# Row softmax on one core: two tiles loaded as one transfer, two stored as one, in a common block of DRAM rows

## The chip, the core and the metric

The kernel runs on one core of one Trainium2 chip; the other cores take no part. The metric is the device time in microseconds (us) from start to end of one execution.

## The reference

```python
def reference(x):                       # x: 16 x 1024 x 512, float32
    x_scaled = x / 2.0
    x_max = np.max(x_scaled, axis=-1, keepdims=True)
    exp_x = np.exp(x_scaled - x_max)
    return (exp_x / np.sum(exp_x, axis=-1, keepdims=True)).astype(np.float32)
```

That is 16,384 rows of 512 numbers, 2 KB a row, 33.55 MB in and 33.55 MB out. Each row is softmaxed by itself.

## The kernel before

The 128 partitions take 128 rows each. A partition's 128 rows are cut into ten tiles, numbered from 0, of 3, 5 and then eight times 15 rows (`TILES`, line 10: rows and the place in `arena`). `arena` is the only data buffer in SBUF, 98 rows per partition; load, exponential, product and store all work in place in it. The tiles 0 to 7 fill it, and the tiles 8 and 9 are laid over tiles 0 to 3 once those are stored.

Three lists say how tiles share DRAM and transfers. `BLOCKS` says which tiles share a block of DRAM rows: within a block of r rows per partition, partition p holds r rows one after the other (`dram`, line 78), so a tile's piece per partition is contiguous and the pieces of neighbouring partitions stand r rows apart. `LOADS` says which tiles are one load (line 130), `STORES` which are one store (line 153); before, `STORES` is `BLOCKS`. A transfer is 128 pieces, one per partition: 15 rows are 30,720 bytes, 30 rows are 61,440.

Who issues what:

- SP issues the load of tile 0, ACT's queue the loads of tiles 1 to 7, all in the first microseconds and without a wait. They run in that order.
- POOL issues the two late loads (`LATE`, line 18). It waits until the exponentials of all tiles before row 83, which are the tiles 0 to 6, are done (line 192, `TURN`), then for the first two stores (tiles 0 and 1, and tile 2) before it loads tile 8, and for the third (tile 3) before it loads tile 9; `LATE` maps a load's number to the numbers of the stores that it newly waits for.
- SP issues all stores in order (lines 229 to 233, `store` at line 150). Before the first it waits until tile 2 has been multiplied; before the second it waits until the first has landed; and each waits until the last tile in it has been multiplied. The landed stores set the semaphores that POOL waits for; the last but one sets `s_near`.

The computation does not subtract the maximum. ACT takes exp(x/2) of one row per partition per instruction, and adds up the row's sum on the way (line 222 for tile 0, line 292 in a loop over chunks of 5 rows for the others). It waits (line 156, `take`) for a count that PE passes on as each load lands (line 209). DVE forms reciprocals (line 182) and multiplies (line 185), 15 rows at a time, and 5 rows at a time in the last tile. At the end, all sums are tested to lie within bounds (POOL line 196, DVE lines 200 and 204, PE line 214); if one does not, a second program over the whole input runs, which it does not do for this input. SP's last waits (lines 277 and 278) are for the last stores.

So there is a load queue (ACT's, then POOL's) and a store queue (SP's), which meet in the same 16 DMA engines.

Of the kernel before, what the change touches and what calls it, by code (L numbers as in the profile page):

```python
# [10 lines left out]
    (3, 0), (5, 3), (15, 8), (15, 23), (15, 38), (15, 53), (15, 68), (15, 83), (15, 0), (15, 15),  # L11
]

BLOCKS = [(0, 1), (2,), (3,), (4,), (5,), (6, 7), (8, 9)]
LOADS = [(0,), (1,), (2,), (3,), (4,), (5,), (6,), (7,), (8,), (9,)]
STORES = BLOCKS

LATE = {8: (0, 1), 9: (2,)}
ARENA = 98

HEAD = [3]
# [11 lines left out]
def kernel(  # L33
# [36 lines left out]
    def span(ts):  # L70
        assert all(tiles[u][2] == tiles[t][2] + tiles[t][1] for t, u in zip(ts, ts[1:]))
        return tiles[ts[0]][0], sum(tiles[t][1] for t in ts), tiles[ts[0]][2]

    for part in (BLOCKS, LOADS, STORES):
        assert [t for ts in part for t in ts] == list(range(len(tiles)))
    loaded = [span(ts) for ts in LOADS]

    def dram(ap, ts):
        b, r, _ = span(ts)
        first, rows, _ = next(span(us) for us in BLOCKS if ts[0] in us)  # L80
        assert first <= b and b + r <= first + rows
        block = ap[first * P : (first + rows) * P].rearrange("(p r) d -> p r d", r=rows)
        return block[:, b - first : b - first + r]

    def sb(ts):
        _, r, at = span(ts)
        return arena[:, at : at + r, :]
# [18 lines left out]
    ld = [nc.alloc_semaphore(f"ld{k}") for k in range(len(loaded))]  # L106
    s_home = {k: nc.alloc_semaphore(f"s_home{k}") for k in LATE}
    s_near = nc.alloc_semaphore("s_near")
# [19 lines left out]
    def load(eng, k):  # L128
        ts = LOADS[k]
        eng.dma_start(out=sb(ts), in_=dram(xf, ts)).then_inc(ld[k], 16)  # L130

    stored_by = {j: s_home[k] for k, js in LATE.items() for j in js}
    for k, (_, r, at) in enumerate(loaded):
        over = {
            j for j, ts in enumerate(STORES)
            if any(
                u < LOADS[k][0] and tiles[u][2] < at + r and at < tiles[u][2] + tiles[u][1]
                for u in ts
            )
        }  # L140
        assert over <= {j for v, js in LATE.items() if v <= k for j in js}

    def landings(js):
        return 16 * len(list(js))

    near = len(STORES) - 2
    sem_of = {**stored_by, near: s_near}
    at_end = landings(j for j in range(len(STORES)) if j not in sem_of)

    def store(eng, j):  # L150
        ts = STORES[j]
        eng.wait_ge(s_mul, upto[ts[-1]])
        eng.dma_start(out=dram(of, ts), in_=sb(ts)).then_inc(sem_of.get(j, s_end), 16)
# [19 lines left out]
    def loads():  # L173
        for k in range(2, min(LATE)):
            load(nc.scalar, k)

    def program():
# [14 lines left out]
        nc.gpsimd.wait_ge(s_exp, starts.index(TURN))  # L192
        for k, js in LATE.items():
            nc.gpsimd.wait_ge(s_home[k], landings(js))
# [13 lines left out]

        for k, ts in enumerate(LOADS):
            nc.tensor.wait_ge(ld[k], 16).then_inc(  # L210
# [17 lines left out]

        nc.sync.wait_ge(s_mul, upto[STORES[FIRST][-1]])
        for j in range(len(STORES)):  # L230
            if j == FIRST:
                nc.sync.wait_ge(s_home[min(LATE)], landings(range(j)))
            store(nc.sync, j)
# [109 lines left out]
```

## Time and profile before

| | |
|---|---|
| median of three runs | 159.79 us (159.79 to 159.9) |
| the profiled execution: its time, its span | 159.81 us, 158.5 us |
| ACT busy | 80.4 us (51%) |
| DVE busy | 73.2 us (46%) |
| DMA records, bytes moved | 2448, 67.11 MB |
| load queue of ACT (q10) | 24.90 MB |
| store queue of SP (q1, with the load of tile 0) | 34.34 MB |
| load queue of POOL (q0) | 7.86 MB |

The span goes from the first to the last instruction of the core; the time has 1.3 us more around it. In the profile's lines PE is TensorE, DVE VectorE, ACT ScalarE, POOL GpSimd, SP SyncE; a q behind an engine's name is its sequencer, which issues transfers and waits. L130 is line 130 of the kernel. A row of 40 digits cuts the span, or the window asked for, in 40 equal slices; each digit is the busy share in tenths. A record (the profile says packet) is one piece of a transfer on one DMA engine.

### The profile page before, as it was taken

To read this page: it belongs to the slowest core of one execution; us is meant where nothing else is said; L and a number is where in the kernel's file an instruction comes from. 1 tells how busy PE (TensorE), PEld (TensorE's weight loads), DVE (VectorE), ACT (ScalarE), POOL (GpSimd) and SP (SyncE) were. 2 spreads that over 40 slices of the span, in tenths; PEclk is the share of its full clock that TensorE was granted. 3 is DMA by queue.
4 is the path that set the end of the run, shared out by engine and by line. 5 is a ranking of instruction groups with operands and counts; after the bars stand their busy time and mean duration, and the time that the engine had idled before them with its cause. 6 is when DMAs were issued, how large, how long until landed. Compare 5 with 4: busy or idle time off the path is not lost. (4 is left out here: it accounts for less than half of the span.)

```text
span 158.5 us, 654 instructions
## 1 busy us (share of the span) xinstructions
PE 0.2 (0%) x2; PEld 0.1 (0%) x2; DVE 73.2 (46%) x27; ACT 80.4 (51%) x257; POOL 2.2 (1%) x8
## 2 busy tenths in 40 slices
PE   0000000000000000000000000000000000000000
PEld 0000000000000000000000000000000000000000
DVE  0056003989989369459500991005964990000000
ACT  0690799999929938940399000894029900000000
POOL 0000000000000000000100010000000010000000
DMA  6999999999998999999999999999999996999695
GB/s 235 442 473 395 473 395 473 395 473 399 412 447 380 466 411 434 434 427 442 419 450 403 465 403 465 403 465 403 465 403 465 496 496 279 465 496 481 295 465 248
DMA packets 2448, 67.11 MB, mean 424 GB/s; under 512 B 272, under 2 KB 272, under 8 KB 400
## 3 DMA queue, kind: packets, MB, share of 16 engines
q1 hardware_dynamic: 1152, 34.34, 50.5%
q10 hardware_dynamic: 1008, 24.90, 36.9%
q0 software_dynamic: 288, 7.86, 11.5%
HBM read 33.55 MB, written 33.55 MB: 424 GB/s over the span
## 5 line engine op out<-in xcount | busy, mean ns | idle before, releaser
L292 ACT ACTIVATE arena<-arena x125 | 76.6, 614 | 41.4 <-ACTq L156 41.4
L185 DVE TENSOR_TENSOR arena<-arena,recip 128x7680 f32<-128x7680 f32 (+2 forms) x12 | 70.2, 5847 | 0.4
L182 DVE RECIPROCAL recip<-stats 128x15 f32<-128x15 f32 (+2 forms) x12 | 2.7, 224 | 56.8 <-ACT arena L292 48.3
L292 ACT ACTIVATION_READ_ACCUMULATOR arena<-arena x125 | 23.4, 187 | 0.0
L218 ACT ACT_TABLE_LOAD x1 | 1.3, 1283 | 4.7 <-issue 4.7
L130 POOL DMA_DIRECT2D arena<-in_x_dram x2 | 1.3, 630 | 89.1 <-DMA out_dram<-arena 89.1
L222 ACT ACTIVATE arena<-arena 128x512 f32<-128x512 f32 x3 | 1.9, 618 | 0.5 <-ACTq L156 0.5
L196 POOL TENSOR_SCALAR inside<-stats 128x128 f32<-128x128 f32 x1 | 0.6, 629 | 35.0 <-ACT arena L292 35.0
L222 ACT ACTIVATION_READ_ACCUMULATOR arena<-arena 128x1 f32 x3 | 0.6, 185 | 0.0
L214 PE MATMUL total<-ones,count 128*1 128x1 f32 x2 | 0.2, 164 | 130.3 <-DVE inside L200 130.3
L200 DVE SCALAR_TENSOR_TENSOR inside<-inside,stats 128x128 f32<-128x128 f32 x1 | 0.3, 283 | 0.0
L204 DVE TENSOR_SCALAR flag<-total 1x1 int32<-1x1 f32 x1 | 0.1, 145 | 0.3 <-PE total L214 0.3
L214 PEld LDWEIGHTS total<-ones,count 128*1 128x1 f32 x2 | 0.1, 80 | 130.3 <-DVE inside L200 130.3
L191 POOL MEMSET ones<- 128x1 f32 x1 | 0.1, 98 | 1.1 <-POOLq L41 1.1
L327 POOL MEMSET const-float32-0.0<- 128x1 f32 x1 | 0.1, 104 | 0.2 <-issue 0.2
L327 POOL MEMSET const-bfloat16-1.0<- 128x1 bf16 x1 | 0.1, 107 | 0.0
L327 POOL MEMSET const-uint8-127<- 128x1 uint8 x1 | 0.1, 107 | 0.0
L327 POOL MEMSET const-float32-1.0<- 128x1 f32 x1 | 0.1, 104 | 0.0
L200 DVE DVE_READ_ACCUMULATOR inside<-inside,stats 128x1 f32 x1 | 0.1, 82 | 0.0
## 6 DMA issues: line engine op xcount, KB each, us to landing
arena<-in_x_dram ACTq DMA_DIRECT2D x6, 3840.0 KB, 38.2
out_dram<-arena SPq DMA_DIRECT2D x4, 3840.0 KB, 45.9
out_dram<-arena SPq DMA_DIRECT2D x2, 7680.0 KB, 36.4
arena<-in_x_dram POOLq DMA_DIRECT2D x2, 3840.0 KB, 24.5
out_dram<-arena SPq DMA_DIRECT2D x1, 2048.0 KB, 19.0
arena<-in_x_dram ACTq DMA_DIRECT2D x1, 1280.0 KB, 7.3
arena<-in_x_dram SPq DMA_DIRECT2D x1, 768.0 KB, 6.3
```

What stands on the lines that cost most here:

```text
L130: eng.dma_start(out=sb(ts), in_=dram(xf, ts)).then_inc(ld[k], 16)
L182: nc.vector.reciprocal(out=recip[:, b : b + c], in_=stats[:, b : b + c])._wait_ge(s_exp, ks[-1] + 1).then_inc(s_rec, 1)
L185: nc.vector.tensor_mul(out=arena[:, a : a + c], in0=arena[:, a : a + c], in1=recip[:, b : b + c].unsqueeze(2).to_broadcast([P, c, D]),)._w ...
L191: nc.gpsimd.memset(ones[:, :], 1.0).then_inc(s_ones, 1)
L196: nc.gpsimd.tensor_scalar(out=inside[:, :], in0=stats[:, :], scalar1=LO, scalar2=HI, op0=Alu.max, op1=Alu.min,)._wait_ge(s_exp, len(sizes) ...
L200: nc.vector.scalar_tensor_tensor(out=inside[:, :], in0=inside[:, :], scalar=1.0, in1=stats[:, :], op0=Alu.mult, op1=Alu.is_equal, accum_ou ...
L204: nc.vector.tensor_scalar(out=flag[:, :], in0=total[:, :], scalar1=float(N), scalar2=None, op0=Alu.is_ge,)._wait_ge(s_tot, 1).then_inc(s_f ...
L214: nc.tensor.matmul(total[:, :], lhsT=count[:, :], rhs=ones[:, :], start=True, stop=True)._wait_ge(s_cnt, 2).then_inc(s_tot, 1)
L218: nc.scalar.preload_act_table(Exp)
L222: ins = nc.scalar.activation(out=arena[:, b], in_=arena[:, b], func=Exp, scale=0.5, accum_out=stats[:, b : b + 1],)
L292: ins = nc.scalar.activation(out=data, in_=data, func=Exp, scale=0.5, accum_out=stats[:, r : n_rows - E + 1 + r][:, bass.ds(now, 1)],)
L327: nc = _bacc.Bacc("TRN2", target_bir_lowering=False, num_devices=1)
```

## The change

The tiles 3, 4 and 5 (the 4th to 6th) come to share one block of 45 DRAM rows per partition. Tiles 3 and 4 are loaded as one transfer of 30 rows, tile 5 by itself; tile 3 is stored by itself, tiles 4 and 5 as one transfer of 30 rows. `LATE` names the same two tiles and the same stores by their new numbers. The places in `arena`, the chunks of ACT and DVE, and all else stay.

```diff
-BLOCKS = [(0, 1), (2,), (3,), (4,), (5,), (6, 7), (8, 9)]
-LOADS = [(0,), (1,), (2,), (3,), (4,), (5,), (6,), (7,), (8,), (9,)]
-STORES = BLOCKS
-
-LATE = {8: (0, 1), 9: (2,)}
+BLOCKS = [(0, 1), (2,), (3, 4, 5), (6, 7), (8, 9)]
+LOADS = [(0,), (1,), (2,), (3, 4), (5,), (6,), (7,), (8,), (9,)]
+STORES = [(0, 1), (2,), (3,), (4, 5), (6, 7), (8, 9)]
+
+LATE = {7: (0, 1), 8: (2,)}
```

## The prediction
> **What bounds the kernel now.** I read the page first, then the queue's transfers stretch by stretch, then the order of issues.
>
> ```profile
> span 158.5 us, 654 instructions
> ...
> DMA  6999999999998999999999999999999996999695
> ...
> DMA packets 2448, 67.11 MB, mean 424 GB/s; under 512 B 272, under 2 KB 272, under 8 KB 400
> ...
> HBM read 33.55 MB, written 33.55 MB: 424 GB/s over the span
> ```
>
> ACT is busy for 51% of the span and DVE for 46%, but the DMA engines are full from the second slice to the last but one. 17 transfers make 17 x 144 = 2448 records: 128 with data (one per partition, so 8 on each of 16 engines) and 16 of 4 bytes that report completion (17 x 16 = 272). The bytes never rest, so the bound is 67.11 MB at the engines' rate plus a start and an end of about a microsecond each. Such a kernel gains little from any change that leaves the bytes alone; it loses if the engines run dry. So the question is whether the stream still holds.
>
> Windows of the DMA view, the first at 40 to 52 us (load queue q10 carries tile 5, then 6; store queue q1 carries the 8 rows of tiles 0 and 1), the second at 60 to 72 us, where both carry 15-row records, the third at 122 to 139 us, stores of 30 rows alone:
>
> ```profile
> q10 hardware_dynamic: 119, 3.16, 62.0%
> q1 hardware_dynamic: 121, 1.87, 36.3%
> ```
>
> ```profile
> q10 hardware_dynamic: 85, 2.61, 50.4%
> q1 hardware_dynamic: 80, 2.46, 47.4%
> ```
>
> ```profile
> q1 hardware_dynamic: 112, 6.88, 93.4%
> ```
>
> Columns: records, MB, share of the 16 engines' time. Two facts come out. Queues with work take turns one record at a time, whatever its size: 119 against 121 records, while the bytes stand 3.16 to 1.87, because a load record is 30 KB and a store record 16 KB. And a record's price: a 30 KB one takes 0.504 x 12 us x 16 / 85 = 1.138 us, a 60 KB one 0.934 x 17 x 16 / 112 = 2.268 us. Size decides the share of a queue.
>
> Now the order (timeline, then issue to landing from the DMA view):
>
> ```profile
> 75.95 0.73 POOL L130 DMA_DIRECT2D arena<-in_x_dram  x1 [74.28 <-DMA out_dram<-arena]
> 91.53 0.53 POOL L130 DMA_DIRECT2D arena<-in_x_dram  x1 [14.84 <-DMA out_dram<-arena]
> 95.73 0.33 SPq L153 DMA_DIRECT2D out_dram<-arena  x1
> 117.71 0.63 ACT L292 ACTIVATE arena<-arena  x1 [8.90 <-ACTq L156]
> 130.11 0.33 SPq L153 DMA_DIRECT2D out_dram<-arena  x1
> ```
>
> ```profile
> arena<-in_x_dram POOLq DMA_DIRECT2D x1, 3840.0 KB, 25.8
> ```
>
> ```profile
> out_dram<-arena SPq DMA_DIRECT2D x1, 7680.0 KB, 44.5
> ```
>
> POOL loads tile 8 and tile 9. Tile 9, issued at 91.53, lands 25.8 later, at 117.3; ACT starts on it at 117.71, and the last store is issued at 130.11, 12.8 us after the landing. The store ahead of it (tiles 6 and 7, issued at 95.73) lands at 95.73 + 44.5 = 140.2. So the last store waits 10.1 us in the queue: that is the whole slack between the last tile's arrival and dry engines.
>
> **The change part by part.**
>
> *Fewer records.* Two merged transfers turn 2 x 8 pairs of records per engine into 60 KB ones: 16 x (2 x 1.138 - 2.268) = 0.13 us, and two completions fewer. This lies on the full stream: -0.15 us at most; I take -0.1, since an idle stretch later absorbs part of it. One issue fewer on ACT (0.3 to 0.65 us) ends before tile 0 lands, and is worth nothing.
>
> *Tiles 3 and 4 land together.* Tile 3 landed at 25.7 (1.95 + 23.7), tile 4 at 34.8 (2.46 + 32.3); now both land at 34.8. ACT took tile 3 up at 26.1 and starts it at about 35.1 instead: 9 us later. With 9.19 us a tile (26.09 to 35.27), tile 3 ends at 44.3, tile 4 at 53.5, tile 5 at 62.7, tile 6 at 71.9 (before 68.9). Tile 7 arrives at 77.6, so ACT has caught up by then. DVE ends tile 3 at 44.3 + 0.3 + 8.2 = 52.8, tile 5 at 71.1. What waits: the first store's gate is tile 2, unchanged. SP's store of tile 3 stood ready behind the landing of the first store at 53.7, so 52.8 still suffices; had it been late, it would be wanted only when tile 2's store lands at 75.3 (53.72 + 21.6). POOL's wait for tile 6's exponentials ends at 71.9, before the 75.3 it waits for anyway: 3.4 us of cover. Cost: 0, and beyond the cover 1 us per us.
>
> *The store of tiles 4 and 5.* It waits on SP for tile 5 (71.1), with only the tiles 6-7 and 8-9 stores behind it, and it is needed when tile 3's store is through: that landed at 54.11 + 37.1 = 91.2. Cover 20 us; cost of the wait 0. POOL's two waits ask for the same tiles' stores as before; up to 91.2 all records are as they were.
>
> *The share of the two queues.* This is the cost. From 91.2 on, SP's records are 60 KB (tiles 4-5, then 6-7, already issued at 95.73), while POOL's are still 30 KB. Before, tile 9's load landed 26.1 us after 91.2: 26.1 / 1.138 = 23 turns, alternating, 12 of stores and 11 of loads. Now the same 12 store turns cost 12 x (2.268 - 1.138) = 13.6 us more. They are there to be had: tiles 4-5 give 8 per engine, tiles 6-7 the other 4. So tile 9 lands at 117.3 + 13.6 = 130.9, tile 8 some 4 us later than before, which ACT's idle time takes up.
>
> *The end.* From 130.9 the chain of ACT and DVE is the one of before: last store issued at 130.9 + 12.8 = 143.7. The stores ahead of it run out at about 140 as before, since the engines moved the same bytes without a gap. So the 10.1 us of slack become a hole: 13.6 - 10.1 = 3.5 us, and a store into empty engines begins later than one queued behind another. The nearest row is the span's own start: first transfer issued at 0.00, first records from 1.0 us on, others by 1.6; I take 1.2 (store 0, issued at 34.68 behind queued loads, shows its first records near 38.5; the engines are empty here, so I stay with the start). Then 8 x 2.268 = 18.1, and 0.5 from the last completion record (157.9) to the end (158.5). Sum: 143.7 + 1.2 + 18.1 + 0.5 = 163.5, less 0.1 = 163.4 of span; the profiled run took 159.81 for a span of 158.46, so + 1.35: **164.8 us**. That run stands at the median (159.79).
>
> Strided DRAM rows, 30 KB pieces in blocks of 45 rows, cost nothing: tiles 6 to 9 are already loaded as 30 KB pieces out of 60 KB blocks at the same 1.138 us.
>
> The Trainium skill (DMA: Bandwidth & Descriptors, section "SWDGE vs HWDGE vs iDMA") describes a packet as preferably at most 4096 B and as the boundary at which an engine switches queues. If so, both queues would get equal bytes whatever a record's size; the 119 to 121 records with 3.16 to 1.87 MB speak against it.
>
> **The rivals.**
>
> *Equal bytes.* If a 60 KB record is cut where queues switch, the shares stay half and half, tile 9 lands at 117.3, and only the fewer records count: 159.8 - 0.15 = 159.6, no slower than before. For it: no stretch shows 60 KB stores beside loads, since 122 us lies behind the last load. Against it: the 16 KB stretch, and one trace record of 60 KB at one steady price. It decides if tile 9 lands before 127.4 (117.3 + 10.1). Chance 0.07.
>
> *A fixed price per transfer.* If each transfer held the engines for a fixed time, two fewer would gain it. The trace bounds this: between 30-row stores the shares leave no gap (437 GB/s through 122 to 140), and single-queue loads ran at 100.5% share. A gain above 0.3 us would have to come from stray slow records, such as the ones when stores first join at 37 us; 159.3. Chance 0.05. The same page of the Trainium skill (section "Anatomy of one DMA") gives about 2.0 us of fixed cost per DMA; by that alone two fewer would be 155.8, below what full engines can move, as most of that cost is latency and here hidden.
>
> *Late compute.* If the 30-row load came more than 3.4 us late, POOL's load of tile 8 slips too and tile 9 with it, 1 us per us: above 167.5 once it is 6 us late. Against it: the load queue is alone until 34.7 and full. Chance 0.04.
>
> **How the numbers follow.** The forecast has 0.84. Its inner uncertainty is the phase of turns and the cold start: 11 or 13 store records instead of 12 move tile 9's landing by one 60 KB record, 2.3 us either way; a first record 3.9 us after its issue, as store 0 had, adds 2.7. So 162.5 to 167.5. These hold the 8 in 10 that are wanted, with the equal-byte case left out. What a measurement can tell from no change is about 0.2%, 0.32 us. Slower: 0.84 + 0.04 = 0.88; same: 0.07 of equal bytes; faster: 0.05.
>
> **What would show it.** Right: 15 x 144 = 2160 records; ACT idle before about 35.1 rather than 26.1; from 91 to 118 us SP moving twice POOL's bytes at equal records; tile 9's exponentials starting near 131; the last store issued near 143.7, with a dip of the DMA row to nearly 0 for some 5 us before it. Wrong: tile 9 still at 117.7 (equal bytes), or no dip although it is late, or the last store issued before 140.

## The result, and the profile after

The changed kernel is slower: 165.33 us in the median of six runs (164.65 to 166.7), against 159.9 us before in the same session; the ratio is 1.036 with a 95% interval of 1.029 to 1.042. The forecast was 164.8 us, in a range of 162.5 to 167.5. Three runs stand at 164.65 to 164.82, the others at 165.85, 166.65 and 166.70; the profiled execution is one of the latter, with 166.65 us for a span of 165.3 us. Some executions of most kernels here run longer and are left out of the ratios and of the times given for each run (13 of 55 of the kernel before, at 163.0 to 164.0 us, which is where three of the four times of the mirror image below lie, and two of four of the store alone, near 173.9 us).

The page of the changed kernel, the lines that answer to those of before:

```profile
span 165.3 us, 651 instructions
...
DMA  7999979989999989989999889889899695059995
...
DMA packets 2160, 67.11 MB, mean 406 GB/s; under 512 B 240, under 2 KB 240, under 8 KB 368
...
HBM read 33.55 MB, written 33.55 MB: 406 GB/s over the span
```

2160 records are 15 x 144, as the change promises, for the same bytes. The row of DMA digits now has a hole near its end, ahead of the last store. (A slice is a fortieth of 165.3 us, 4.1 us.) The order of issues, from the timeline, with the late load's and the last store's time from issue to landing from the DMA view:

```profile
90.47 0.53 POOL L130 DMA_DIRECT2D arena<-in_x_dram  x1 [13.69 <-DMA out_dram<-arena]
95.89 0.33 SPq L153 DMA_DIRECT2D out_dram<-arena  x1
133.38 0.63 ACT L292 ACTIVATE arena<-arena  x1 [19.91 <-ACTq L156]
145.78 0.33 SPq L153 DMA_DIRECT2D out_dram<-arena  x1
```

```profile
arena<-in_x_dram POOLq DMA_DIRECT2D x1, 3840.0 KB, 42.6
```

```profile
out_dram<-arena SPq DMA_DIRECT2D x1, 7680.0 KB, 19.5
```

Tile 9's load is issued at 90.47, a microsecond earlier than before, but takes 42.6 us instead of 25.8 and lands at 133.0 instead of 117.3. The last store is issued at 145.78 instead of 130.11, and lands 19.5 us later instead of 28.3: it no longer queues, it starts on empty engines. How empty they were, from the table by stretches (columns: stretch, length, busy time of PE, PEld, DVE, ACT and POOL, clock, DMA share, GB/s; a record counts where it starts):

```profile
140.00:146.00 6.00, 0.00 (x0) 0.00 (x0) 5.92 (x5) 2.67 (x10) 0.63 (x1) 1.00 0.00 0
```

And the reason, from the DMA view of the changed kernel between 119.4 and 130 us, where POOL's load of tile 9 (q0) runs beside SP's store of tiles 6 and 7 (q1):

```profile
q1 hardware_dynamic: 48, 2.95, 64.2%
q0 software_dynamic: 48, 1.47, 32.2%
```

The two queues move the same number of records and one moves twice the bytes. That is the turn-taking by record that the forecast rested on, now with 60 KB against 30 KB.

### The profile page after: what moved, and what is told of

The parts are those of the page before. It is cut to its first block, busy times and chain, and to the rows that moved or that the text cites. A ratio compares the mean times of both kernels' runs of the same rounds, so it can differ in the third digit from the quotient of the medians.

```text
span 165.3 us, 651 instructions
## 1 busy us (share of the span) xinstructions
PE 0.2 (0%) x2; PEld 0.1 (0%) x2; DVE 73.2 (44%) x27; ACT 80.3 (49%) x257; POOL 2.2 (1%) x8
## 2 busy tenths in 40 slices
DMA packets 2160, 67.11 MB, mean 406 GB/s; under 512 B 240, under 2 KB 240, under 8 KB 368
## 6 DMA issues: line engine op xcount, KB each, us to landing
out_dram<-arena SPq DMA_DIRECT2D x3, 7680.0 KB, 46.2
```

## The experiments

The theory to be tested: on each DMA engine the queues take turns by record, so the 60 KB records of the merged store starve the 30 KB records of tile 9's load; the rest of the change costs nothing. Rivals: the late start of ACT on tile 3, the strided DRAM block, or the merged transfer as such. All kernels are timed against the kernel before, which gave 159.85 to 159.92 us in the median in these sessions.

**Store alone.** The ten loads of before are put back; the shared block and the merged store stay.

```diff
 # changed kernel, with
-LOADS = [(0,), (1,), (2,), (3, 4), (5,), (6,), (7,), (8,), (9,)]
+LOADS = [(0,), (1,), (2,), (3,), (4,), (5,), (6,), (7,), (8,), (9,)]
-LATE = {7: (0, 1), 8: (2,)}
+LATE = {8: (0, 1), 9: (2,)}
```

> The shared block and the merged store of tiles 4 and 5, with the ten loads of before. Theory (the DMA engines take turns by record, so 60 KB store records starve tile 9's 30 KB load): all of the loss is here, tile 9's first exponential near 131 to 133 us, last store issued 144 to 146, time 164.7 to 166.7 us, a hole in the DMA row ahead of the last store. Rival (the loss comes from tiles 3 and 4 landing together and ACT starting 9 us late): 159.8 us.

Measured: 164.84 and 164.67 us, tile 9's first exponential at 131.49, last store issued at 143.89 (timeline):

```profile
131.49 0.63 ACT L292 ACTIVATE arena<-arena  x1 [18.09 <-ACTq L156]
143.89 0.33 SPq L153 DMA_DIRECT2D out_dram<-arena  x1
```

Without the merged load, both times are at the level of the changed kernel's three shorter runs (164.65 to 164.82 us), so the merged load has no part in that loss. This run also hits the sum of the prediction closely: 130.9 forecast for the landing, 131.1 measured (90.42 + 40.7), 143.7 forecast for the last issue, 143.89 measured.

**Load alone.** The merged load and the shared block stay, tiles 3, 4 and 5 are stored one by one.

```diff
 # changed kernel, with
-STORES = [(0, 1), (2,), (3,), (4, 5), (6, 7), (8, 9)]
+STORES = [(0, 1), (2,), (3,), (4,), (5,), (6, 7), (8, 9)]
```

> The shared block and the merged load of tiles 3 and 4, with one store each for tiles 3, 4 and 5. Theory of turns by record: no record of 60 KB meets a late load before 117 us, so tile 9's first exponential is at 117.7 us as before and the time is 159.7 us (0.07 us of records saved), although ACT starts tile 3 at 35 instead of 26 us. Rival (late start of ACT, or DRAM rows in a block of 45): 164.7 us or a part of the 5 us.

Measured: 159.79 us, ratio 1.0003 (0.9993 to 1.0012). Tile 9's first exponential stands at 117.73. ACT's late start on tile 3 and the block of 45 rows are free, and the fewer records bring nothing that can be measured.

**The same transfers, small records.** This is the run that separates a transfer's size from its records' size. The tiles 3, 4 and 5 keep blocks of their own; a merged transfer walks two blocks, with the tile as an extra dimension of its pattern.

```diff
 # changed kernel, with
-BLOCKS = [(0, 1), (2,), (3, 4, 5), (6, 7), (8, 9)]
+BLOCKS = [(0, 1), (2,), (3,), (4,), (5,), (6, 7), (8, 9)]
 # in dram(), for a transfer over several blocks
+            both = ap[b * P : (b + r) * P]
+            return both.rearrange("(t p r) d -> p t r d", t=len(ts), p=P)
 # in sb(), likewise
+            return arena[:, at : at + r, :].rearrange("p (t r) d -> p t r d", t=len(ts))
```

> The same two merged transfers (7680 KB each, the same waits), but tiles 3, 4 and 5 keep blocks of their own, so that a transfer is 256 pieces of 30,720 bytes instead of 128 of 61,440. Theory of turns by record: equal records, equal shares, tile 9 at 117.7 us, time 159.8 us. Rival (the size of the transfer, its waits or the order of landings makes the loss, whatever its records): 164.7 us.

Measured: 159.71 us, ratio 1.0001 (0.9991 to 1.001). The store of tiles 4 and 5 is issued as late as in the changed kernel, at 71.30, as one transfer of 7680 KB. The DMA view from 92 to 115 us:

```profile
q1 hardware_dynamic: 176, 5.41, 54.4%
q0 software_dynamic: 161, 4.45, 44.9%
```

All data records are of 30 KB (16 of q0's are the 4-byte completions), the bytes stand nearly level, and tile 9 starts at 119.07: 1.4 us later than forecast, well within the slack. So neither the number of transfers nor their waits nor the order of landings makes the loss.

**Fewer large turns.** The changed kernel, with the store of tiles 6 and 7 in two, so that 8 and not 12 store turns are of 60 KB.

```diff
 # changed kernel, with
-STORES = [(0, 1), (2,), (3,), (4, 5), (6, 7), (8, 9)]
+STORES = [(0, 1), (2,), (3,), (4, 5), (6,), (7,), (8, 9)]
```

> The changed kernel with the store of tiles 6 and 7 cut into two of 15 rows, so that only the 8 store records per engine of tiles 4 and 5 are of 60 KB, not 12 of those that tile 9's load meets. Theory: tile 9 lands 8 x 1.13 = 9.0 us later than before, at 126.4, last store issued near 139.2, just before the stores ahead of it run out at 140: time 159.7 to 160.9 us, nearly all of the loss gone though the merged store stays. Rival (the merged store as such, or the load of tiles 3 and 4, costs the 5 us): 164.7 us.

Measured: 161.76, 161.37 and 161.40 us, ratio 1.010 (1.008 to 1.012). Some two thirds of the loss is gone with the merged store still there, which the rival does not allow; but the rest is larger than expected. Tile 9 landed at 128.15 (90.45 + 37.7) instead of 126.4, although 15 of the 16 engines reported before 126.2. The window from 126.2 to 128.2 us shows the one that did not:

```profile
q0 software_dynamic: 1, 0.00, 0.0%
```

**Small load records, no merged store.** The kernel before, each of POOL's late loads cut in two.

```diff
 # kernel before, in load()
+        if k in LATE:
+            half = 8
+            for lo, hi in ((0, half), (half, span(ts)[1])):
+                eng.dma_start(out=sb(ts)[:, lo:hi], in_=dram(xf, ts)[:, lo:hi]).then_inc(ld[k], 16)
+            return
 # and PE waits for both pieces
-            nc.tensor.wait_ge(ld[k], 16).then_inc(
+            nc.tensor.wait_ge(ld[k], 32 if k in LATE else 16).then_inc(
```

> The kernel before, all stores as they were, but each of POOL's two late loads cut into one of 8 and one of 7 rows, so that its records are 16 and 14 KB (about 0.57 us) and 16 per engine and tile. Theory of turns by record: the loads' share falls without any merged store. From 81 us on each load record waits for a store record: 19 turns with 30 KB stores (1.138 + 0.573), then 8 with the 60 KB store of tiles 6 and 7 (2.268 + 0.573), then 5 alone: tile 9 lands near 139.5 instead of 117.3, last store issued near 152.3, time about 173 us. Rival (shares go by bytes, or only a merged store can do harm): 159.8 to 160.5 us.

Measured: 176.6, 176.5 and 175.28 us, ratio 1.10 (1.09 to 1.11). Tile 9's second half landed at 142.9 (88.89 + 54.0), 3.4 us beyond the forecast; 14 engines had reported it before 140, and two were late. The window from 96 to 110 us:

```profile
q1 hardware_dynamic: 151, 4.15, 68.9%
q0 software_dynamic: 144, 1.87, 31.2%
```

Equal records again, 2.2 to 1 in bytes. A loss of the same kind, three times as large, comes without the merged store of tiles 4 and 5: what sets the shares is the ratio of the record sizes.

**The mirror image.** The kernel before, with the stores of tiles 3, 4 and 5 cut in two.

```diff
 # kernel before, in store(), with HALVED = (2, 3, 4) of STORES
-        eng.dma_start(out=dram(of, ts), in_=sb(ts)).then_inc(sem_of.get(j, s_end), 16)
+        for lo, hi in ((0, 8), (8, 15)) if j in HALVED else ((0, span(ts)[1]),):
+            eng.dma_start(out=dram(of, ts)[:, lo:hi], in_=sb(ts)[:, lo:hi]).then_inc(
+                sem_of.get(j, s_end), 16
+            )
 # and the waits for a store in two pieces count 32 completions instead of 16
```

> The mirror image: the kernel before, but the stores of tiles 3, 4 and 5 are each cut into one of 8 and one of 7 rows, so that the store records are the small ones beside POOL's 30 KB loads. Theory: the loads get two thirds of the engines, tile 9 lands near 108 to 111 us instead of 117.3, and the time stays at 159.8 us, because the engines were full and an earlier tile 9 only waits longer behind the stores. Rival (tile 9's arrival still bounds the kernel before): faster than 159.8 by up to 5 us.

Measured: 161.8 to 163.31 us, ratio 1.019 (1.011 to 1.027). Neither side had that. Tile 9 landed at 115.1 only, because its load was issued at 96.40, after late pieces of tile 3's store, and the end was late too: from 158.6 us on, when the kernel before has ended, two records of 60 KB were still to begin.

```profile
DMA packets 4, 0.12 MB, mean 37 GB/s; under 512 B 2, under 2 KB 2, under 8 KB 2
```

Four records, two with data and two completions: two engines ended 3.5 us later than the kernel before (a span of 162.0 against 158.5). So this run says nothing yet on the question that it was made for, and whether the cut stores cause its late end is not shown. The next asks it again with less.

```diff
 # kernel of the mirror image, with
-HALVED = (2, 3, 4)
+HALVED = (3, 4)
```

> As the run with halved stores, but only the stores of tiles 4 and 5 are cut into 8 and 7 rows; tile 3 is stored in one piece, so that POOL's load of tile 9 is not held back by late pieces of tile 3's store, and two transfers instead of three are added. Theory: from 91 us on the loads have two thirds of the engines (8 x (1.138 + 0.573) = 13.7 us a tile), tile 8 lands near 97, tile 9 near 111 us instead of 117.3, and the time is 159.8 us, since earliness is worth nothing. If instead small store records beside loads hold single engines up, as two engines were in that run, those engines end last and the time is 161 to 163 us.

Measured: 159.81 us, ratio 1.0001 (0.999 to 1.0012). Tile 9 landed at 111.1 (92.53 + 18.6), 6 us earlier than in the kernel before, and the last store was issued at 123.89 instead of 130.11. The window from 97 to 110 us and the issue:

```profile
q0 software_dynamic: 128, 3.93, 70.0%
q1 hardware_dynamic: 126, 1.66, 29.9%
```

```profile
123.89 0.33 SPq L156 DMA_DIRECT2D out_dram<-arena  x1
```

The share has turned round and the time has not moved. Nor do small store records beside loads, by themselves, hold engines up: the 161 to 163 us of that case did not come. An earlier tile 9 is worth nothing while the engines are full; a later one is paid for as soon as the slack is used up.

**A repair that keeps the merged store.** The changed kernel, with the store of tiles 6 and 7 in four pieces.

```diff
 # changed kernel, with the loop over pieces of the mirror image in store(), and
-STORES = [(0, 1), (2,), (3,), (4, 5), (6, 7), (8, 9)]
+STORES = [(0, 1), (2,), (3,), (4, 5), (6,), (7,), (8, 9)]
+HALVED = (4, 5)
 # and the waits for a store in two pieces count 32 completions instead of 16
```

> The changed kernel, merged load and merged store of tiles 4 and 5 kept, with the store of tiles 6 and 7 cut into four of 8, 7, 8 and 7 rows. Theory: the 8 turns with 60 KB store records stay, but the 4 turns after them meet 16 KB records: 4 x (2.268 - 0.611) = 6.6 us less than in the changed kernel, so tile 9 lands near 124.3 us (126.3 if one engine is 2 us late again), the last store is issued before the stores ahead run out at 140, and the time is 159.8 to 160.6 us. Rival (the merged store does harm of its own): 163 us or more.

Measured: 159.86 to 162.18 us in nine runs, ratio 1.008 (1.003 to 1.012). Three runs are at 159.86 to 160.03, six at 161.28 to 162.18. In the profiled one (161.28) tile 9 landed at 125.8 (91.79 + 34.0) and 14 of the engines had reported it by 123.9; the last store, issued in time (138.57), ended on two engines 1.3 and 1.6 us after the others. The mechanism is repaired, the lag is not, and the version is no gain on the kernel before.

No version beat the kernel before: the three that tie with it (159.71, 159.79 and 159.81 us) have between 2304 and 2736 records and full DMA engines to the end.

## Why the prediction was right

**The bound.** Full DMA engines: the three ties show that neither one or two transfers fewer nor an earlier tile 9 buys anything.

**Fewer records, -0.1 us.** The load alone should have gained 0.07 us and measured +0.03%, interval -0.07% to +0.12%; too small to tell, as said.

**Tiles 3 and 4 landing together, 0.** ACT started tile 3 at 34.96 (35.1 forecast); tile 5 was multiplied and its store issued at 71.13 (71.1). POOL's load of tile 8 was issued at 76.06 where before it was 75.95. The cover held, and the load-alone run shows the price as nothing.

**The share of the queues, +13.6 us on tile 9.** Tile 9 was to land at 130.9. In the store-alone run it landed at 131.1, and the turns are those of the forecast. From 90.9 to 130.7 us that run shows:

```profile
q1 hardware_dynamic: 208, 11.80, 68.4%
q0 software_dynamic: 206, 5.41, 31.6%
```

The bytes are 192 records of 60 KB and 176 of 30 KB (the other records report completions), so 12 of stores and 11 of loads on each of the 16 engines. In the profiled run of the changed kernel 15 engines reported completion between 130.0 and 130.6 us, and one between 130.6 and 133.1 (POOL's queue in these two windows):

```profile
q0 software_dynamic: 15, 0.00, 1.4%
```

```profile
q0 software_dynamic: 1, 0.00, 0.0%
```

A tile is usable when the last engine has reported, so that one engine cost 2 us. The profile does not name the engines, but the order of the records tells what held this one up. In the window of 0.1 us at 116.2 stands one record of 30 KB at 178.0% of 16 engines for 0.1 us, that is 2.85 us instead of 1.138:

```profile
q0 software_dynamic: 1, 0.03, 178.0%
```

It ends near 119.08, and in the window from 118.5 to 119.3 us only one record with data starts, beside one completion; both start there:

```profile
q0 software_dynamic: 1, 0.03, 8.9%
q1 hardware_dynamic: 1, 0.00, 0.1%
```

From there each record of this engine starts where the one before it ended, and the row of them leads to the last completion of tile 9, at 132.67. One record of 60 KB on the same engine, at 110.28, took 2.55 us instead of 2.268. The two together are 2.0 us over their price, which is nearly all of the lag. Why these two were slow, no run tells.

This is the part that the forecast did not have. Its range held it only through the allowance for the phase of turns, which is another cause of the same size.

**The end.** 12.8 us from landing to last issue: 133.0 to 145.78. A store on empty engines was put at 1.2 + 18.1 + 0.5 = 19.8 us and took 19.5; its first records, one on each engine, start between 146.6 and 146.8, 0.8 us after the issue, so the 1.2 was 0.4 us too much. In the store-alone run tile 9 and the last issue came 0.2 us later than forecast; the two misses cancel in part, so that 164.8 forecast and 164.84 us measured agree this closely is in part luck. The store of tiles 6 and 7 was to end at about 140: in the store-alone run it landed at 140.2 (95.82 + 44.4), in the profiled run of the changed kernel at 142.1 (95.89 + 46.2), on the engine that lagged.

**The rivals.** Equal bytes per queue is refuted by every window above in which the queues' records differ in size; so is the Trainium skill's packet of preferably at most 4096 B as the boundary of a turn (DMA: Bandwidth & Descriptors, section "SWDGE vs HWDGE vs iDMA") for transfers like these: 48 records of 60 KB took turns with 48 of 30 KB. A fixed price per transfer that the full engines would have to pay is refuted by the small-records run, which has two transfers fewer and the time of before. Late compute did not occur.

## What to carry to other kernels

When two queues share full DMA engines, as here with records of 14 to 60 KB, the size of a queue's records, not of its transfers, sets its share: give the larger records to the queue whose landing is awaited, and the smaller to the one that only has to drain. Before merging transfers, ask which other queue runs beside them and what waits for it; here 12 turns at 1.13 us each ate a slack of 10.1 us. This kernel, whose engines are already full, had nothing to gain from such a merge (ratios 1.0003 and 1.0001), and a layout that makes a neighbour's rows contiguous changes the record size unasked.

## What the runs showed of the hardware beyond that

One or two of the sixteen DMA engines fall behind by 1.3 to 3.3 us in some of the kernels with unequal records: one by 2.2 us in the changed kernel and by 1.7 us in the fewer-large-turns run, two by 1.3 and 1.6 us in the repair, two by up to 3 us in the run with small load records, two by 3.2 and 3.3 us in the mirror image. In the store alone, the load alone, the small records and the second mirror image the last engine reports tile 9 within 0.4 us of the fourteenth. In the changed kernel two slow records account for it, as shown above; in the fewer-large-turns run a record of 30 KB that starts between 116.3 and 116.4 us took 2.32 us:

```profile
q0 software_dynamic: 1, 0.03, 145.2%
```

That a lag of this kind makes the two groups of times of one kernel (164.7 and 166.7; 159.9 and 161.6) fits its size, but is not shown, since there is one profile of each kernel. Which engines these are, and what slows them, no run here tells; it stays open.
